# Differential scores in four row groups, operand transposes by single bank, a 96-row block in the query expansion

## The chip, the cores and the metric

The kernel runs on one core of a Trainium2 chip. The metric is the device time of one execution in microseconds (us). Engines are named as the profile has them: PE is TensorE, DVE is VectorE, ACT is ScalarE, POOL is GpSimd, SP is SyncE.

## What is computed

A hybrid encoder trunk of two layers works on two groups of 256 tokens of 1024 channels that share all parameters. Each layer projects the normed input into columns for four token mixers "a" to "d" and their gates, runs the mixers, merges them by sigmoid gates, projects, and ends in a gated MLP. The change touches the differential mixer "a", the operands of "c" and "d", and the query expansion of "c":

```python
def diff_mixer(cols, ang, lq1, lk1, lq2, lk2, subln, lam_init):
    q, k, v = jnp.split(cols, [A_QK_COLS, 2 * A_QK_COLS], axis=-1)
    q = apply_rope(q.reshape(b, s, A_HEADS, 2, A_D), ang) * (A_D ** -0.5)
    k = apply_rope(k.reshape(b, s, A_HEADS, 2, A_D), ang)
    ...
        sc = jnp.einsum('bqhcd,bkhcd->bhcqk', qb, k).astype(f32)
        p = jax.nn.softmax(sc, axis=-1)
        w = (p[:, :, 0] - lam * p[:, :, 1]).astype(v.dtype)
        return jnp.einsum('bhqk,bkhd->bqhd', w, v)
    o = rmsnorm(o, subln) * (1.0 - lam_init)
...
def mla_mixer(cols, ang, q_norm, kv_norm, w_uq, w_ukv):
    cq, ckv, k_rope = jnp.split(cols, [C_QLORA, C_QLORA + C_KVLORA], axis=-1)
    q = (rmsnorm(cq, q_norm) @ w_uq).reshape(b, s, C_HEADS, C_NOPE + C_ROPE)
```

There are four "a" heads with two score maps each, of width A_D = 32; C_QLORA is 192, that is 128 rows and 64.

## The kernel before

Every fp32 matmul is made of three fp32r matmuls on split operands: a value is written as a high part `h` and a low part `l`, and a product is hh + hl + lh (`mm3`, L297 to L299). The weights come in 264 pieces: an SP queue loads `raw`, ACT rounds it to `wh` (L289), and DVE and POOL share the rest `wl` (L292, L293). 512 tokens, both groups, lie in the free dimension.

The work is a list of units, one for a column of weights, in the order b, a, d, c of the mixers and then the gates; a unit's matmuls take a PSUM bank (`psum`), and an evacuation follows a unit later. Side generators run a step at a time between units. `pair_gen(mix, b, j)` handles one pair of heads of one group: scores, softmax, transposes of the probabilities (`pt`, L808) and their evacuation (`ptr`, L814), then the product with the values (`po`, L862). `cd_gen` makes the operands of "c" and "d" from token-major columns by transposing them on TensorE (L558). The program order of all this is then rearranged by a scheduler, so which instruction stands before which on an engine is seen only in the order of the built kernel.

PSUM has 8 banks of 512 columns: `pm` has four, for all main products (`psak`, `psva`, `psvd`, `pg`, `tr`, `cq`); `psx` two, for scores (`sc`); `pst` one, for `pt`; `pso` one, for `po`. A bank's next use waits until its last reader is done.

- *Mixer "a".* `a_evac` takes a finished product of 128 rows (four maps of 32), rotates it (`rc`, `rsh`, POOL has a part), splits it into `h` and `l`, and then stacks, for each of the four maps, three 32-row slices into one 96-row operand (`aq0p`, ...): h, h, l for queries against h, l, h for keys, so that one matmul of 96 rows gives all three terms. Of the 12 slice copies of an operand, four go to ACT (`APACK`, L604) and eight to DVE (L606). The scores of a head's two maps are 2 matmuls each (L738), and the two heads of a pair follow at different steps.
- *Mixers "b" and "d"* use `scores_rows` (L755 to L766): two heads lie in rows 0 to 63 and 64 to 127, and their 12 matmuls alternate between the two row groups (L765). "b" adds a bias on DVE right from the score bank (`sb`, L776).
- *The query expansion* `cq_pe` (L635 to L637) multiplies per 128 tokens a 128-row block and a 64-row block (`c0`, `c1`) of 384 columns.
- POOL also makes row tables for "d" (`rt`, from L474 on), at the time of the "b" pairs.

Of the kernel before, what the change touches and what calls it, by code (L numbers as in the profile page):

```python
# [30 lines left out]
APACK = (0, 3, 6, 9)  # L31
# [171 lines left out]
def trunk_kernel(ctx: ExitStack, tc: tile.TileContext, xt, wflat, gains, lams, rpb, consts, yt):  # L203
# [232 lines left out]
    def build_layer(l):  # L436
# [85 lines left out]
        def cd_gen():  # L522
# [30 lines left out]
            for i in range(0, 6, 2):  # L553
                pss = []
                for nm, src, a, m, g in jobs[i:i + 2]:
                    ps = psum("tr")
                    for t in range(4):
                        PE.transpose(out=ps[:m, t * 128:t * 128 + 128], in_=att[src][t][:, a:a + m], identity=ident)  # L558
                    pss.append(ps)
                yield  # L560
                for ps, (nm, src, a, m, g) in zip(pss, jobs[i:i + 2]):
                    h, lo = t2(nm + "h", F32R), t2(nm + "l", F32R)
                    if g is None:
                        split(ps[:m], h[:m], lo[:m])
                    else:
                        gc = gcol(l, g, 0, m)
                        S.activation(out=h[:m], in_=ps[:m], func=AF.Copy, scale=gc)
                        V.scalar_tensor_tensor(out=lo[:m], in0=ps[:m], scalar=gc, in1=f(h[:m]), op0=ALU.mult,
                                               op1=ALU.subtract)
                    att[nm] = (h, lo)  # L570
                yield
# [16 lines left out]
        def a_evac(nm):  # L588
            def evac():
                ps = D.pop(nm)  # L590
                c, sh = t2("rc"), t2("rsh")
                V.tensor_tensor(out=c, in0=ps, in1=st["cosr"], op=ALU.mult)
                V.stream_shuffle(out=sh, in_=ps, mask=SWAP)
                G.tensor_tensor(out=sh, in0=sh, in1=st["sinr"], op=ALU.mult)
                V.tensor_tensor(out=c, in0=c, in1=sh, op=ALU.add)
                h, lo = t2(nm + "h", F32R), t2(nm + "l", F32R)
                split(c, h, lo)
                parts = (h, h, lo) if nm[1] == "q" else (h, lo, h)
                for m in range(4):
                    pk = t2(f"{nm}p{m}", F32R)  # L600
                    r = slice(32 * m, 32 * m + 32)
                    for i, src in enumerate(parts):
                        if (3 * m + i) % 12 in APACK:
                            S.activation(out=pk[32 * i:32 * i + 32], in_=f(src[r]), func=AF.Copy)  # L604
                        else:
                            V.tensor_copy(out=pk[32 * i:32 * i + 32], in_=f(src[r]))  # L606
                    att[nm, m] = pk
# [19 lines left out]
        def cq_pe(wh, wl):  # L627
            w = [a[:, :768].rearrange("p (k c) -> p k c", k=2) for a in (wh, wl)]
            att["cqr"] = []
            for t in range(4):  # L630
                ps = psum("cq")
                o = ps[:, :384]
                for k, m in ((0, 128), (1, 64)):
# [87 lines left out]
        def heads(mix, j):  # L721
            if mix == "a":
                return [[((f"aq{j}", 2 * e + c), (f"ak{j}", 2 * e + c), 0, 96) for c in range(2)] for e in range(2)]
# [8 lines left out]
        def scores(maps, b):  # L732
            out = []
            for qn, kn, p0, n in maps:
                ps = psum("sc", psx)
                if isinstance(qn, tuple):
                    for qt in range(2):
                        PE.matmul(ps[:, qt * 256:qt * 256 + 256],  # L738
                                  lhsT=att[qn][0:96, b * 256 + qt * 128:b * 256 + qt * 128 + 128],
                                  rhs=att[kn][0:96, b * 256:b * 256 + 256], start=True, stop=True)  # L740
                    out.append(ps)
                    continue
# [12 lines left out]
        def scores_rows(maps, b):  # L755
            pss = [psum("sc", psx) for _ in maps]
# [75 lines left out]
        def pair_gen(mix, b, j):  # L832
            hs = heads(mix, j)
            rows = mix in "bd"
            if rows:
                s0, s1 = ([ps] for ps in scores_rows([hs[0][0], hs[1][0]], b))
# [456 lines left out]
```

## Time and profile before

| | |
|---|---|
| time, median of 3 runs | 1647.43 us (1647.31 to 1648.04) |
| the profiled execution, its own time | 1647.62 us |
| span of its trace | 1645.8 us |
| mean granted clock of TensorE | 0.989 |
| busy: PE / DVE / POOL / ACT | 1615.6 / 1003.9 / 663.1 / 634.9 us |

The span is the time from the first to the last instruction in the trace. A matmul's busy time includes its way through the array, so the matmuls of a full pipe overlap in the listing, and the distance of two starts says how long one occupies the engine. A granted clock of 1.00 is the 2.4 GHz level, 0.50 the 1.2 GHz level. A figure in brackets behind an instruction is the idle time of its engine just before it, and what ended it.

### The profile page before, as it was taken

What the parts mean: (1) busy time and instruction counts of PE and PEld (TensorE: products, weight loads), DVE (VectorE), ACT (ScalarE), POOL (GpSimd) and SP (SyncE); (2) the same over time, 40 slices, a digit from 0 to 9 for tenths busy, and PEclk for the clock granted to TensorE, in tenths of its full rate; (3) what the DMA queues carried; (4) which work ended last, traced back from release to release, by engine and by line L of the source; (5) the groups of instructions that cost most, each with busy time, mean ns of one, the idle gap of its engine ahead of it and who ended that gap; (6) DMA issues with size and microseconds to landing.
All of it is one profiled execution on the core that took longest, in us unless ns stands there. A gap on an engine that the chain in (4) does not pass through costs nothing.

```text
span 1645.8 us, 21201 instructions
## 1 busy us (share of the span) xinstructions
PE 1615.6 (98%) x8035; PEld 1343.8 (82%) x8035; DVE 1003.9 (61%) x1668; ACT 634.9 (39%) x1115; POOL 663.1 (40%) x449
## 2 busy tenths in 40 slices
PE   8989999999999999999998999999999999999997
PEld 6889877878888888888886987888788888888886
DVE  7787585655776666633358675756468666656113
ACT  4555553342323333322234554544333333333321
POOL 4352223444634444444444312234465344444342
PEclk9999999999999999999998999999999999999999
DMA  6222122222323322323331121322222233232331
GB/s 218 84 68 82 55 96 80 80 78 70 107 90 103 98 95 91 98 93 106 101 109 67 55 94 57 108 84 80 77 72 98 90 103 103 90 98 88 106 95 63
DMA packets 50534, 149.24 MB, mean 91 GB/s; under 512 B 13184, under 2 KB 16128, under 8 KB 50432
## 3 DMA queue, kind: packets, MB, share of 16 engines
q1 hardware_dynamic: 49344, 146.84, 27.4%
q8 instruction: 63, 1.03, 0.3%
q10 hardware_dynamic: 1088, 1.05, 0.2%
q14 instruction: 39, 0.32, 0.1%
HBM read 145.77 MB, written 2.10 MB: 90 GB/s over the span
## 4 chain that ended last, share of the span: by engine, by line
PE 93%; DVE 3%; issue 2%; ACT 1%; POOL 0%; DMA 0%; SPq 0%; POOLq 0%; ACTq 0%; DVEq 0%
PE pf L298 10%; PE pf L299 10%; PE pf L297 10%; PE pg L297 7%; PE pg L298 7%; PE pg L299 7%; PE pfo L297 5%; PE pfo L298 5%; PE pfo L299 5%; PE pb L299 2%; PE pwo L299 2%; PE pb L298 2%; PE pwo L298 2%; PE pb L297 2%; PE pwo L297 2%
## 5 line engine op out<-in xcount | busy, mean ns | idle before, releaser
L293 POOL TENSOR_TENSOR wl<-raw,wh 128x512 fp32r<-128x512 f32 (+4 forms) x264 | 449.9, 1705 | 561.7 <-ACT wh L289 439.9
L289 ACT ACTIVATE wh<-raw 128x1024 fp32r<-128x1024 f32 (+5 forms) x264 | 281.7, 1068 | 436.4 <-PE pfo L298 132.3
L292 DVE TENSOR_TENSOR wl<-raw,wh 128x512 fp32r<-128x512 f32 (+4 forms) x262 | 254.1, 970 | 213.6 <-ACT wh L289 203.6
L297 PE MATMUL pf<-xh,wh 128*128 128x512 f32 x704 | 274.3, 390 | 0.0
L299 PE MATMUL pf<-xh,wl 128*128 128x512 f32 x704 | 273.9, 389 | 0.0
L298 PE MATMUL pf<-xl,wh 128*128 128x512 f32 x704 | 273.9, 389 | 0.0
L297 PE MATMUL pg<-xh,wh 128*128 128x512 f32 x512 | 202.2, 395 | 0.1
L298 PE MATMUL pg<-xl,wh 128*128 128x512 f32 x512 | 199.8, 390 | 0.0
L299 PE MATMUL pg<-xh,wl 128*128 128x512 f32 x512 | 199.5, 390 | 0.0
L297 PEld LDWEIGHTS pf<-xh,wh 128*128 128x128 f32 x704 | 132.2, 188 | 27.5
L298 PEld LDWEIGHTS pf<-xl,wh 128*128 128x128 f32 x704 | 132.2, 188 | 27.4
L299 PEld LDWEIGHTS pf<-xh,wl 128*128 128x128 f32 x704 | 132.2, 188 | 27.2
L297 PE MATMUL pfo<-ah,wh 128*128 128x512 f32 (+1 forms) x374 | 141.1, 377 | 0.0
L298 PE MATMUL pfo<-al,wh 128*128 128x512 f32 (+1 forms) x374 | 140.8, 376 | 0.0
L299 PE MATMUL pfo<-ah,wl 128*128 128x512 f32 (+1 forms) x374 | 140.8, 376 | 0.0
L931 POOL TENSOR_TENSOR mg<-mg,gz 128x512 f32<-128x512 f32 x48 | 64.5, 1347 | 165.4 <-DVE gz L930 165.4
L303 POOL TENSOR_TENSOR al<-fc,ah 128x512 fp32r<-128x512 f32 x44 | 57.8, 1314 | 178.9 <-ACT ah L302 178.9
L297 PEld LDWEIGHTS pg<-xh,wh 128*128 128x128 f32 x512 | 96.2, 188 | 21.1 <-issue 0.9
L299 PEld LDWEIGHTS pg<-xh,wl 128*128 128x128 f32 x512 | 96.1, 188 | 20.5
L298 PEld LDWEIGHTS pg<-xl,wh 128*128 128x128 f32 x512 | 96.3, 188 | 18.3
L952 ACT ACTIVATE gz<-gz 128x512 f32<-128x512 f32 x64 | 40.4, 631 | 127.3 <-DVE gz L951 127.2
L788 ACT ACTIVATE pr<-sc,mx 128x256 f32<-128x256 f32 x128 | 59.1, 471 | 78.6 <-DVE mx L783 78.6
(390 smaller groups left out, 2917.5 us busy)
## 6 DMA issues: line engine op xcount, KB each, us to landing
raw<-in_w_dram SPq DMA_DIRECT2D x158, 512.0 KB, 3.3
raw<-in_w_dram SPq DMA_DIRECT2D x58, 640.0 KB, 3.8
raw<-in_w_dram SPq DMA_DIRECT2D x32, 448.0 KB, 3.3
raw<-in_w_dram SPq DMA_DIRECT2D x4, 576.0 KB, 3.4
bias<-in_rpb_dram SPq DMA_DIRECT2D x32, 64.0 KB, 3.5
xall<-in_xt_dram SPq DMA_DIRECT2D x3, 512.0 KB, 7.1
raw<-in_w_dram SPq DMA_DIRECT2D x4, 256.0 KB, 4.5
out_dram<-y SPq DMA_DIRECT2D x4, 256.0 KB, 2.5
```

The source lines that it names most:

```text
L289: S.activation(out=wh[:, a:b], in_=raw[:, a:b], func=AF.Copy)
L292: V.tensor_tensor(out=wl[:, a:c], in0=raw[:, a:c], in1=f(wh[:, a:c]), op=ALU.subtract)
L293: G.tensor_tensor(out=wl[:, c:b], in0=raw[:, c:b], in1=f(wh[:, c:b]), op=ALU.subtract)
L297: PE.matmul(ps, lhsT=wh, rhs=xh, start=first, stop=False)
L298: PE.matmul(ps, lhsT=wh, rhs=xl, start=False, stop=False)
L299: PE.matmul(ps, lhsT=wl, rhs=xh, start=False, stop=last)
L303: (eng or V).tensor_tensor(out=l, in0=v, in1=f(h), op=ALU.subtract)
L788: S.activation(out=p[:, qt * 256:qt * 256 + 256], in_=src[c][:, qt * 256:qt * 256 + 256], func=AF.Exp, scale=sc, bias=mx[:, i:i + 1], accu ...
L931: G.tensor_tensor(out=m, in0=m, in1=z, op=ALU.add)
L952: S.activation(out=z, in_=z, func=AF.Tanh, scale=0.5)
```

## The change

`a_evac` stops at the split `h` and `l`; the stacked operands and their copies are gone. The scores of an "a" pair go through `scores_rows`: four maps, each in its own 32 rows, take 24 matmuls (3 terms, 2 query tiles, 4 maps) in one go. The banks of maps 0 and 1 come from `psx`, those of maps 2 and 3 from `pm`. `cd_gen` transposes and splits its six operands one at a time, each in a step of its own, instead of two at a time. The second block of `cq_pe` has 96 rows; the added rows meet weights that are zero. The functions touched stand in a diff of the source:

```diff
--- before.py
+++ after.py
@@ -28,7 +28,6 @@
 RPB_W = 128
 ORD = 'badc'
 GSEQ = [(i, d) for i in ('abcd'.index(m) for m in ORD) for d in range(ND)]
-APACK = (0, 3, 6, 9)
 NWARM = 9
 BLAG = 5
 GX = [(25, 29), (31, 32)]
@@ -550,24 +549,20 @@
                 yield
             jobs = (("dk", "dr", 288, 128, None), ("dq0", "dr", 32, 128, None), ("dq1", "dr", 160, 128, None),
                     ("c2", "cf", 0, 128, G_CKV), ("c0", "cf", 128, 128, G_CQ), ("c1", "cf", 256, 96, G_CQ + 1))
-            for i in range(0, 6, 2):
-                pss = []
-                for nm, src, a, m, g in jobs[i:i + 2]:
-                    ps = psum("tr")
-                    for t in range(4):
-                        PE.transpose(out=ps[:m, t * 128:t * 128 + 128], in_=att[src][t][:, a:a + m], identity=ident)
-                    pss.append(ps)
+            for nm, src, a, m, g in jobs:
+                ps = psum("tr")
+                for t in range(4):
+                    PE.transpose(out=ps[:m, t * 128:t * 128 + 128], in_=att[src][t][:, a:a + m], identity=ident)
                 yield
-                for ps, (nm, src, a, m, g) in zip(pss, jobs[i:i + 2]):
-                    h, lo = t2(nm + "h", F32R), t2(nm + "l", F32R)
-                    if g is None:
-                        split(ps[:m], h[:m], lo[:m])
-                    else:
-                        gc = gcol(l, g, 0, m)
-                        S.activation(out=h[:m], in_=ps[:m], func=AF.Copy, scale=gc)
-                        V.scalar_tensor_tensor(out=lo[:m], in0=ps[:m], scalar=gc, in1=f(h[:m]), op0=ALU.mult,
-                                               op1=ALU.subtract)
-                    att[nm] = (h, lo)
+                h, lo = t2(nm + "h", F32R), t2(nm + "l", F32R)
+                if g is None:
+                    split(ps[:m], h[:m], lo[:m])
+                else:
+                    gc = gcol(l, g, 0, m)
+                    S.activation(out=h[:m], in_=ps[:m], func=AF.Copy, scale=gc)
+                    V.scalar_tensor_tensor(out=lo[:m], in0=ps[:m], scalar=gc, in1=f(h[:m]), op0=ALU.mult,
+                                           op1=ALU.subtract)
+                att[nm] = (h, lo)
                 yield
 
         def swap_h():
@@ -595,16 +590,7 @@
                 V.tensor_tensor(out=c, in0=c, in1=sh, op=ALU.add)
                 h, lo = t2(nm + "h", F32R), t2(nm + "l", F32R)
                 split(c, h, lo)
-                parts = (h, h, lo) if nm[1] == "q" else (h, lo, h)
-                for m in range(4):
-                    pk = t2(f"{nm}p{m}", F32R)
-                    r = slice(32 * m, 32 * m + 32)
-                    for i, src in enumerate(parts):
-                        if (3 * m + i) % 12 in APACK:
-                            S.activation(out=pk[32 * i:32 * i + 32], in_=f(src[r]), func=AF.Copy)
-                        else:
-                            V.tensor_copy(out=pk[32 * i:32 * i + 32], in_=f(src[r]))
-                    att[nm, m] = pk
+                att[nm] = (h, lo)
             return evac
 
         def b_evac(nm):
@@ -630,7 +616,7 @@
             for t in range(4):
                 ps = psum("cq")
                 o = ps[:, :384]
-                for k, m in ((0, 128), (1, 64)):
+                for k, m in ((0, 128), (1, 96)):
                     h, lo = (a[:m, t * 128:t * 128 + 128] for a in att[f"c{k}"])
                     PE.matmul(o, lhsT=h, rhs=w[0][:m, k], start=(k == 0), stop=False)
                     PE.matmul(o, lhsT=h, rhs=w[1][:m, k], start=False, stop=False)
@@ -720,7 +706,7 @@
 
         def heads(mix, j):
             if mix == "a":
-                return [[((f"aq{j}", 2 * e + c), (f"ak{j}", 2 * e + c), 0, 96) for c in range(2)] for e in range(2)]
+                return [[(f"aq{j}", f"ak{j}", 32 * (2 * e + c), 32) for c in range(2)] for e in range(2)]
             if mix == "b":
                 return [[(f"bq{j}", f"bk{j}", 64 * e, 64)] for e in range(2)]
             if mix == "c":
@@ -733,13 +719,6 @@
             out = []
             for qn, kn, p0, n in maps:
                 ps = psum("sc", psx)
-                if isinstance(qn, tuple):
-                    for qt in range(2):
-                        PE.matmul(ps[:, qt * 256:qt * 256 + 256],
-                                  lhsT=att[qn][0:96, b * 256 + qt * 128:b * 256 + qt * 128 + 128],
-                                  rhs=att[kn][0:96, b * 256:b * 256 + 256], start=True, stop=True)
-                    out.append(ps)
-                    continue
                 (qh, ql), (kh, kl) = att[qn], att[kn]
                 ks = slice(b * 256, b * 256 + 256)
                 p = slice(p0, p0 + n)
@@ -753,7 +732,7 @@
             return out
 
         def scores_rows(maps, b):
-            pss = [psum("sc", psx) for _ in maps]
+            pss = [psum("sc", psx if i < 2 else pm) for i in range(len(maps))]
             ks = slice(b * 256, b * 256 + 256)
             for qt in range(2):
                 qs = slice(b * 256 + qt * 128, b * 256 + qt * 128 + 128)
@@ -831,9 +810,10 @@
 
         def pair_gen(mix, b, j):
             hs = heads(mix, j)
-            rows = mix in "bd"
+            rows = mix in "abd"
             if rows:
-                s0, s1 = ([ps] for ps in scores_rows([hs[0][0], hs[1][0]], b))
+                ss = scores_rows(hs[0] + hs[1], b)
+                s0, s1 = ss[:len(ss) // 2], ss[len(ss) // 2:]
             else:
                 s0 = scores(hs[0], b)
             yield
```

The order of the built kernels shows three places. On VectorE, in the stage of the second "b" head of layer 1, before (`aq1h` and `aq1l` are the split query operand, `sb` the bias addition that frees a score bank, `ob0l` an output's low part):

```order
L303 TENSOR_TENSOR aq1l_848<-rc_841,aq1h_847 128x512
L606 CAST aq1p0_851<-aq1h_847 32x512
L606 CAST aq1p0_851<-aq1l_848 32x512
L606 CAST aq1p1_855<-aq1h_847 32x512
L606 CAST aq1p1_855<-aq1l_848 32x512
L606 CAST aq1p2_859<-aq1h_847 32x512
L606 CAST aq1p2_859<-aq1l_848 32x512
L606 CAST aq1p3_863<-aq1h_847 32x512
L606 CAST aq1p3_863<-aq1l_848 32x512
L303 TENSOR_TENSOR ob0l_875<-po_819,ob0h_874 128x256
L776 SCALAR_TENSOR_TENSOR sb_909<-sc_781,bias3_242 128x512
L592 TENSOR_TENSOR rc_918<-psak1_794,cosr_373 128x512
```

And after, from the line ahead of `aq1l` on:

```order
L777 TENSOR_SCALAR sb_800<-sb_800,ri_799 128x256 x2
L302 TENSOR_TENSOR aq1l_816<-rc_809,aq1h_815 128x512
L291 TENSOR_TENSOR wl12_881<-raw12_683,wh12_880 128x576
L302 TENSOR_TENSOR ob0l_827<-po_787,ob0h_826 128x256
L755 SCALAR_TENSOR_TENSOR sb_861<-sc_749,bias3_242 128x512
L587 TENSOR_TENSOR rc_870<-psak1_762,cosr_373 128x512
```

The eight casts between the query's low part and `sb` are gone; the weight residue `wl12`, which stood ahead of the reciprocal before, now stands there with `ob0l`.

On TensorE, in the gate stage of layer 1 (`pg` a gate column, `tr` a transposed operand in a main bank, `dr` the token-major columns), before:

```order
L298 MATMUL pg_1704<-xl7_169,wh18_1510 128x512
L299 MATMUL pg_1704<-xh7_168,wl18_1511 128x512
L558 MATMUL tr_1754<-cst_82,dr0_896 128x128
L558 MATMUL tr_1754<-cst_82,dr1_897 128x128
L558 MATMUL tr_1754<-cst_82,dr2_898 128x128
L558 MATMUL tr_1754<-cst_82,dr3_899 128x128
L558 MATMUL tr_1759<-cst_82,dr0_896 128x128
L558 MATMUL tr_1759<-cst_82,dr1_897 128x128
L558 MATMUL tr_1759<-cst_82,dr2_898 128x128
L558 MATMUL tr_1759<-cst_82,dr3_899 128x128
L297 MATMUL pg_1764<-xh0_122,wh19_1689 128x512
L298 MATMUL pg_1764<-xl0_123,wh19_1689 128x512
```

And after:

```order
L297 MATMUL pg_1672<-xl7_169,wh18_1462 128x512
L298 MATMUL pg_1672<-xh7_168,wl18_1463 128x512
L555 MATMUL tr_1722<-cst_82,dr0_848 128x128
L555 MATMUL tr_1722<-cst_82,dr1_849 128x128
L555 MATMUL tr_1722<-cst_82,dr2_850 128x128
L555 MATMUL tr_1722<-cst_82,dr3_851 128x128
L296 MATMUL pg_1727<-xh0_122,wh19_1663 128x512
L297 MATMUL pg_1727<-xl0_123,wh19_1663 128x512
L298 MATMUL pg_1727<-xh0_122,wl19_1664 128x512
```

One transposed operand stands between two gate columns instead of two; `pg_1727` takes the main bank that the first "a" pair's last map (`sc_1473`) had.

On TensorE, later in the gate stage of layer 1, around the start of the fourth "a" pair's scores, before (`po` is the product with the values, in two row groups and two key tiles):

```order
L299 MATMUL pg_1982<-xh7_168,wl22_1897 128x512
L862 MATMUL po_2010<-ptr_1819,vA_88 64x256
L862 MATMUL po_2010<-ptr_1903,vA_88 64x256
L862 MATMUL po_2010<-ptr_1819,vA_88 64x256
L862 MATMUL po_2010<-ptr_1903,vA_88 64x256
L808 MATMUL pt_2015<-cst_82,pr_1884 128x128 x4
L738 MATMUL sc_2030<-ak1p0_928,aq1p0_851 128x256 x2
L738 MATMUL sc_2033<-ak1p1_932,aq1p1_855 128x256 x2
L297 MATMUL pg_2036<-xh0_122,wh23_1975 128x512
```

And after:

```order
L787 MATMUL pt_1841<-cst_82,pr_1703 128x128 x4
L555 MATMUL tr_1877<-cst_82,dr0_848 128x128
L555 MATMUL tr_1877<-cst_82,dr1_849 128x128
L555 MATMUL tr_1877<-cst_82,dr2_850 128x128
L555 MATMUL tr_1877<-cst_82,dr3_851 128x128
L842 MATMUL po_1972<-ptr_1778,vA_88 64x256
L744 MATMUL sc_2001<-ak1h_876,aq1h_815 128x256
L744 MATMUL sc_2002<-ak1h_876,aq1h_815 128x256
L842 MATMUL po_1972<-ptr_1875,vA_88 64x256
L842 MATMUL po_1972<-ptr_1778,vA_88 64x256
L296 MATMUL pg_1882<-xh0_122,wh21_1769 128x512
```

Before, the four `po` matmuls stand together and four score matmuls follow; now three `po` matmuls stand around two score matmuls (of 24), the fourth `po` and the other 22 come behind the gate column.

## Rows read from the trace of the kernel before

**Rows 1.** Page, busy time of the engines and their instructions.

```profile
PE 1615.6 (98%) x8035; PEld 1343.8 (82%) x8035; DVE 1003.9 (61%) x1668; ACT 634.9 (39%) x1115; POOL 663.1 (40%) x449
```

**Rows 2.** TensorE's waits: line, releaser, us in total, times, longest.

```profile
PE sc L765 <- DVE sb L776: 9.3, 4, 3.1
PE pt L808 <- ACT ptr L814: 4.4, 2, 2.2
```

**Rows 3.** Timeline, TensorE, layer 1: start, us, instruction, count, idle before and releaser.

```profile
73.14 1.56 PE L862 MATMUL po<-ptr,vB 128*64 128x256 f32 x8
...
74.63 0.66 PE L808 MATMUL pt<-cst,sb 128*128 128x128 f32 x4
...
86.39 0.66 PE L808 MATMUL pt<-cst,sb 128*128 128x128 f32 x4 [2.19 <-ACT ptr L814]
...
90.81 0.58 PE L765 MATMUL sc<-bk1h,bq1h 64*128 64x256 f32 x1 [3.05 <-DVE sb L776]
...
92.98 0.41 PE L457 MATMUL psvd<-wh,xl 128*128 128x256 f32 x1
93.19 0.41 PE L455 MATMUL psvd<-wh,xh 128*128 128x256 f32 x1
...
99.95 1.08 PE L862 MATMUL po<-ptr,vB 128*64 128x256 f32 x8
```

**Rows 4.** Timeline, TensorE, layer 2, the same stretch.

```profile
884.45 0.66 PE L808 MATMUL pt<-cst,sb 128*128 128x128 f32 x4
...
910.88 1.08 PE L862 MATMUL po<-ptr,vB 128*64 128x256 f32 x8
```

**Rows 5.** Windows: busy us of each engine in 5 us, then TensorE's clock.

```profile
90.00:95.00 5.00, 4.19 (x18) 3.97 (x19) 3.50 (x9) 1.57 (x6) 1.28 (x1) 0.50 0.00 0
```

**Rows 6.** VectorE: one group of casts by line; then the timeline.

```profile
L606 DVE CAST aq1p<-aq1h 32x512 fp32r<-32x512 f32 x8 | 5.4, 671 | 0.1
...
90.08 0.68 DVE L776 SCALAR_TENSOR_TENSOR sb<-sc,bias 128x512 f32<-128x512 f32 x1
```

**Rows 7.** Timeline, TensorE, scores among value matmuls.

```profile
135.16 0.28 PE L455 MATMUL psva<-wh,xh 128*128 128x256 f32 x1
135.28 0.28 PE L456 MATMUL psva<-wl,xh 128*128 128x256 f32 x1
135.40 0.44 PE L738 MATMUL sc<-ak0p,aq0p 96*128 96x256 f32 x2
135.68 0.28 PE L457 MATMUL psva<-wh,xl 128*128 128x256 f32 x1
```

**Rows 8.** Chain of waits, TensorE: start, us, name, line, count.

```profile
146.35 0.44 PE pt L808 x4
...
152.74 0.87 PE tr L558 x8
...
161.56 0.48 PE sc L738 x4
...
205.23 0.91 PE sc L765 x12
```

**Rows 9.** Timeline, GpSimd, row tables.

```profile
81.32 0.68 POOL L474 COPY rt<-cst 128x32 f32<-128x32 f32 x1
...
87.84 1.58 POOL L477 TENSOR_TENSOR rt<-cst,lv 128x256 f32<-128x256 f32 x2
```

**Rows 10.** Timeline, TensorE, starts of two blocks of the query expansion.

```profile
206.06 0.44 PE L635 MATMUL cq<-wh,c0h 128*128 128x384 f32 x1
...
206.79 0.44 PE L635 MATMUL cq<-wh,c1h 64*128 64x384 f32 x1
```

**Rows 11.** Timeline, VectorE and ScalarE, softmax of the first "a" pair.

```profile
142.05 0.18 DVE L791 RECIPROCAL ri<-su 128x4 f32<-128x4 f32 x1 [2.48 <-ACT pr L788]
...
153.11 1.28 DVE L782 TENSOR_REDUCE mx<-sc 128x2 f32<-128x512 f32 x2
...
155.70 0.47 ACT L788 ACTIVATE pr<-sc,mx 128x256 f32<-128x256 f32 x1 [2.04 <-DVE mx L783]
```

## The prediction, made before the changed kernel was run

> **What bounds the kernel now.** I read the page first: TensorE is busy for 98% of the span, VectorE for 61% [rows 1]. With an engine that full, a change can only gain where TensorE idles, where it runs slowly, or where work is taken off it, and it can lose wherever a new wait is put ahead of it. So the second view is the table of TensorE's waits. Only two of them are more than a microsecond: score matmuls of the "b" mixer (L765) that wait for `sb` on VectorE, 9.3 us in four waits, and transposes of its probabilities (L808) that wait for `ptr` on ScalarE, 4.4 us in two [rows 2]. The third view, TensorE's timeline, shows where these lie: all in one stretch per layer, between the first "b" pair's transposes and the next `po` group, 74.63 to 99.95 us in layer 1 [rows 3] and 884.45 to 910.88 us in layer 2 [rows 4]. The reader is to see there two more things. The matmuls behind a stall are spaced 0.21 us apart instead of 0.12 us, and the windows give the slice from 90 to 95 us a granted clock of 0.50, which is the 1.2 GHz level [rows 3, 5]. So each stall is paid twice, once idle and once at half clock.
>
> Why does TensorE wait there? The second "b" head needs a score bank of PSUM, of which there are two, and a bank is free only when VectorE has added the bias into `sb`. VectorE does this for the third score bank at 90.08 us [rows 6], and TensorE starts 0.7 us later [rows 3]. Ahead of it in VectorE's queue stand the eight casts that build the stacked operands of `aq1`, those from `aq1h` 0.67 us each on average [rows 6]; the order shown above has the same eight rows between `aq1l` and `sb`.
>
> **The change part by part.**
>
> *The stall of the "b" stage.* The change takes 64 casts off VectorE and 32 copies off ScalarE, four operands of each layer. What TensorE has to do between the two points is 96 matmuls of 256 columns at 0.1195 us [rows 7], or 11.5 us, two groups of scores at 0.91 us and two of transposes at 0.44 us [rows 8], and 0.2 us of small change: 14.4 us. The stretch lasts 25.32 us in layer 1 and 26.43 us in layer 2 [rows 3, 4], so 51.75 − 28.8 = 22.9 us is lost there, 13.7 us of it idle [rows 2] and the other 9.2 us at half clock. If I replay VectorE's queue without the casts, from the same durations, `sb` of the second head is ready near 76.1 us where TensorE wants it near 77.3 us, a margin of 1.2 us. What is late next is GpSimd: its row tables run from 81.32 to 89.4 us [rows 9] and hold its part of the rotary product, so VectorE gets the rotated operand at about 85 us, and the bank of `psvd` comes free at about 88 us where TensorE wants it at 90.6 us. So I expect the whole 22.9 us: **−22.9**. With no wait the first `po` group, which now lasts 1.56 us in one place and 1.08 us in the other [rows 3], should be short in both layers: **−1.0**.
>
> *The query expansion.* In `cq` a block of three 384-column matmuls takes 0.73 us from start to start [rows 10], where at the steady rate it would be 3 × 1.5 × 0.1195 = 0.54 us. It alternates between 128 rows and 64 rows, so each change of form costs about 0.19 us. A 96-row pair in a stream of 128-row matmuls costs no such step: two of them start at 135.40 us and the stream goes on at 135.68 us, 0.28 us for two matmuls [rows 7]. With 96 rows some seven of eight changes go, in two layers: 14 × 0.2 = **−2.8**. The extra rows add no columns.
>
> *The scores.* Eight pairs (four per layer) were two groups of four stacked matmuls, 0.48 us each [rows 8], 0.96 us a pair. Now they are 24 matmuls of 32 rows. The trace has no 32-row groups; the nearest row is two groups of 64 rows, twelve matmuls in 0.91 us with the mode changes, which is six times 0.12 us and 0.2 us: the two groups run beside each other [rows 8]. If four groups run beside each other, 24 matmuls are again six steps, 0.91 us, and I take that: 8 × (0.91 − 0.96) = **−0.4**. The other ends are two at a time, 12 × 0.12 + 0.2 = 1.6 us, and one at a time, 24 × 0.12 + 0.2 = 3.1 us; these are rivals below.
>
> The Trainium skill, "TensorE: Matmul & The Clock Gate", Part 3 (Packing small matmuls), gives 3.07× for four row tiles of K=32, less than the four that I take from the 64-row pair. By it, as an estimate, a pair would be 24 × 0.12 / 3.07 + 0.2 = 1.14 us, and the sum 1.8 us higher; no row here shows four tiles.
>
> *Split groups.* In the new order the fourth "a" pair and the first "d" pair are cut: part of `po`, two or three score matmuls, more of `po`, a whole gate column, and only then the rest. A cut means four more changes of form, of 0.19 us or less, and part of a `po` group that does not overlap: about 0.65 us for each of two places in each layer, **+2.6** (from 0.8 us, if changes overlap, to 4).
>
> *A new wait for a main bank.* Maps 2 and 3 of a pair take their banks from the pool of the main products. In the gate stage `pg` must then have the bank that the first "a" pair's last map held, and that is freed by the exponentials on ScalarE. In before the reciprocal `ri` is at 142.05 us, the maxima `mx` at 153.11 us, and the exponential `pr` at 155.70 us [rows 11], behind VectorE's queue of scalings and weight residues. By the replay of the new order VectorE has both maxima about a microsecond sooner, the two exponentials end near 154.9 us, and TensorE, which has only four transposes there instead of eight (0.87 us for eight [rows 8]), comes at 152.7 us. The wait is then 2.2 us per layer, **+4.4**. It is nothing if VectorE's queue is 2 us shorter than replayed, and 4 us if ScalarE does weights first. What queues behind it on TensorE is everything, since it works in order. After the stalls of the "b" stage the half clock cost 9.2 us for six stalls [rows 2, 5], 1.5 us for one; whether a single stall among full columns brings it is not shown, so I take half of it for two layers, **+1.5** (0 to 3.1). Other small waits for the two main banks that are left (`psva`, `tr`, `pg` alternate on them, with margins of 0.6 to 0.9 us in the replay): **+0.5**.
>
> *The transposes one bank at a time.* They are the same 24 per layer, in six steps instead of three. They end before `cq` starts in either order, so I cost them at nothing; what hides the splitting of each is the gate column in between, 24 matmuls of 512 columns or 24 × 2 × 0.1195 = 5.7 us of TensorE work. Without that cover a transposition wait would be at most the 0.4 us of four transposes a step.
>
> **The sum.** −22.9 − 1.0 − 2.8 − 0.4 + 2.6 + 4.4 + 1.5 + 0.5 = −18.1 us. The profiled execution took 1647.6 us (its span is 1645.8 us), 0.2 us over the median of the runs shown: 1647.6 − 18.1 = **1629.5 us**. Its own range is 1623.5 us, with no wait for the main bank (−4.4 − 1.5), to 1634.7 us, with 4 us each and all of the half clock (+3.6 + 1.6).
>
> **The rivals.**
>
> *A, the main banks become the bound.* Two of four are held by scores through a softmax, and each of two further columns per layer waits some 2 us as well: 1629.5 + 2 × 2 × 1.8 = 1637 us (1634 to 1641). For it: the margins of 0.6 to 0.9 us above. Against it: a column is 5.7 us long, and a bank is wanted once in a column. The Trainium skill, "TensorEngine Tiling (Array Packing)", Gotcha 1 (PSUM Pressure), says that different row tiles write to different banks, so two banks could not do; no run here shows it yet. Chance 0.15.
>
> *B, row groups overlap only two at a time.* 1.6 us instead of 0.91 us in eight pairs: +5.5, 1635 us. The only overlap in the trace is of two [rows 8]. Chance 0.10.
>
> *C, the slower side: row groups run one after another, at the half clock.* Few rows at work could bring the 1.2 GHz level, as the stretch of the stalls has it [rows 5], and at its spacing of 0.21 us [rows 3] a pair would take 24 × 0.21 + 0.2 = 5.2 us: +4.3 × 8 = +34.6, about 1664 us. It decides from 3.2 us a pair (0.91 + 18.1 / 8), where the gain is gone. Against it: 64-row groups overlap [rows 8]. Chance 0.03.
>
> *D, the stall only moves.* GpSimd's row tables [rows 9] or a margin of 1.2 us lost leave one stall of 1.6 to 2 us with its half clock in each layer: +6 to 7, 1636 us. Chance 0.05.
>
> *E, the change doesn't do what it says*: `sb` is late for another reason (weight residues of VectorE), and the casts' time goes to those. About 1647 us. Chance 0.03.
>
> **How the numbers follow.** The forecast has the remaining 0.64. The range from 1622 to 1638 us holds nine tenths of it (0.58), half of A (0.08), B and D: 0.81. Differences within 0.2%, 3.3 us, are about what a measurement of this kernel can tell from none. Faster by more are the forecast, A, B and D, 0.94; the same is E, 0.03; slower is C, 0.03.
>
> **What would show it.** The waits L765 on `sb` and L808 on `ptr` should be gone from the table of waits, and the windows from 75 to 95 us should have clock 1.00; if a wait of over a microsecond stands there, the replay was wrong. In `cq` the blocks should start 0.54 us apart. The 24 score matmuls of an "a" pair should take 0.9 to 1.1 us; 1.6 us is B. A new row `pg <- ACT pr` should stand among the waits, some 2 us long, twice; several of them are A, and none at all would put the time near 1623.5 us.

## The result, and the profile after

The changed kernel takes **1635.91 us** (median of 4 runs, 1633.07 to 1636.70), beside 1647.67 us for the kernel before: a ratio of 0.9925, with a 95% interval from 0.9908 to 0.9943. Measured again in a later group of runs it took 1634.30 us (1632.39 to 1635.81, 5 runs) beside 1647.38 us, 0.9921 (0.9909 to 0.9934). The time is lower by 12 to 13 us, where 18.1 us were forecast; it lies inside the range from 1622 to 1638 us, near its upper end. The forecast's own range, up to 1634.7 us, holds the second of these times and not the first.

The page of the changed kernel, line 1 of busy time (engine, us, share, instructions), answers to [rows 1]. VectorE lost 64 instructions and 36 us; TensorE has more matmuls, and is busy for 99%:

```profile
PE 1612.5 (99%) x8163; PEld 1338.6 (82%) x8163; DVE 968.2 (59%) x1604; ACT 614.2 (38%) x1083; POOL 661.8 (41%) x449
```

TensorE's waits after, the longest sums first (releaser, us in total, times, longest), answer to [rows 2]. Both waits of the "b" stage are gone; on top stands a wait that the kernel before does not have, a gate column for ScalarE's `pr`; the second is the first weights' at the start of the program:

```profile
PE pg L296 <- ACT pr L767: 4.5, 2, 2.3
PE psbk L296 <- ACT wh L288: 2.7, 1, 2.7
```

The windows after over the stretch where the stall was (busy us of each engine, then TensorE's clock) answer to [rows 5]. TensorE is busy throughout, at clock 1.00:

```profile
75.00:80.00 5.00, 5.00 (x38) 4.04 (x35) 4.64 (x10) 1.91 (x4) 3.77 (x6) 1.00 0.15 21
80.00:85.00 5.00, 5.00 (x44) 5.00 (x43) 0.77 (x2) 1.46 (x5) 4.56 (x9) 1.00 0.27 112
...
90.00:95.00 5.00, 5.00 (x41) 4.34 (x40) 4.74 (x10) 3.92 (x10) 3.88 (x3) 1.00 0.32 102
```

Where the time went is read from the starts of five pieces of work on TensorE's timeline: the "b" pair's `po` ahead of the stall, the first `psve`, the first `psva`, the first `cq`, and the gate column behind the query expansion. Layer 1 before (the first and the fourth also stand in [rows 3, 10]):

```profile
101.38 0.38 PE L455 MATMUL psve<-wh,xh 128*128 128x288 f32 x1
...
134.01 0.36 PE L455 MATMUL psva<-wh,xh 128*128 128x256 f32 x1
...
212.17 0.48 PE L297 MATMUL pg<-xh,wh 128*128 128x512 f32 x1
```

And the same pieces of layer 1 after:

```profile
74.47 1.08 PE L842 MATMUL po<-ptr,vB 128*64 128x256 f32 x8
...
91.64 0.38 PE L454 MATMUL psve<-wh,xh 128*128 128x288 f32 x1
...
125.00 0.39 PE L454 MATMUL psva<-wh,xh 128*128 128x256 f32 x1
...
203.24 0.44 PE L621 MATMUL cq<-wh,c0h 128*128 128x384 f32 x1
...
208.22 0.47 PE L296 MATMUL pg<-xh,wh 128*128 128x512 f32 x1
```

The differences of these starts, and of the same ones in layer 2, give the length of each stretch in us:

| stretch | layer 1 before | after | layer 2 before | after |
|---|---|---|---|---|
| `po` to `psve` (the stall) | 28.24 | 17.17 | 29.33 | 17.17 |
| `psve` to `psva` | 32.63 | 33.36 | 32.63 | 33.36 |
| `psva` to `cq` (gate stage) | 72.05 | 78.24 | 72.04 | 76.59 |
| `cq` to the gate column | 6.11 | 4.98 | 6.10 | 4.99 |

So the stall gives 23.2 us and the query expansion 2.2 us, as forecast to within a microsecond; but `psve` to `cq` takes 6.9 us more in layer 1 and 5.3 us more in layer 2, 12.2 us, which is half of the gain. The second and the third row are to be taken together: of the four "a" pairs of a layer the second one's scores, about 1 us, stand behind the first `psva` before and ahead of it after. Everything behind (the rest of the gates, the output, the MLP) is the same to 0.2 us. The first `po` of the profiled execution comes 1.3 us later than before; in the profiles of other kernels here it comes from 72.9 to 74.7 us, in a second profile of the changed kernel at 73.2 us, so this is scatter of the start and no part of the change. Of the 1.3 us some 0.9 us are longer waits for the first weights (2.7 and 0.7 us instead of 1.9 and 0.5 us).

### The profile page after: what moved, and what is told of

The parts are those of the page before. It is cut to its first block, busy times and chain, and to the rows that moved or that the text cites. A ratio compares the mean times of both kernels' runs of the same rounds, so it can differ in the third digit from the quotient of the medians.

```text
span 1633.6 us, 21325 instructions
## 1 busy us (share of the span) xinstructions
PE 1612.5 (99%) x8163; PEld 1338.6 (82%) x8163; DVE 968.2 (59%) x1604; ACT 614.2 (38%) x1083; POOL 661.8 (41%) x449
## 4 chain that ended last, share of the span: by engine, by line
PE 95%; DVE 3%; ACT 1%; issue 1%; DMA 0%; POOL 0%; SPq 0%; POOLq 0%; ACTq 0%; DVEq 0%
PE pf L297 10%; PE pf L296 10%; PE pf L298 10%; PE pg L296 7%; PE pg L297 7%; PE pg L298 7%; PE pfo L296 5%; PE pfo L297 5%; PE pfo L298 5%; PE po L842 2%; PE pt L787 2%; PE pb L298 2%; PE pwo L298 2%; PE pb L296 2%; PE pb L297 2%; PE pwo L297 2%
## 5 line engine op out<-in xcount | busy, mean ns | idle before, releaser
L296 PEld LDWEIGHTS pg<-xh,wh 128*128 128x128 f32 x512 | 96.5, 188 | 28.2 <-ACT pr L767 5.0
```

The lines of the kernel that those rows point to most:

```text
L296: PE.matmul(ps, lhsT=wh, rhs=xh, start=first, stop=False)
```

## The experiments

In the order of the questions: was it the casts, where does the gate stage lose, and what are the other two parts worth. Lengths of stretches are taken from the profiles as in the table above.

**The casts alone put back.** The changed kernel, with the copies of the operands made again (their results are not read):

```diff
                 att[nm] = (h, lo)
+                parts = (h, h, lo) if nm[1] == "q" else (h, lo, h)
+                for m in range(4):
+                    pk = t2(f"{nm}p{m}", F32R)
...
+                            S.activation(out=pk[32 * i:32 * i + 32], in_=f(src[r]), func=AF.Copy)
...
+                            V.tensor_copy(out=pk[32 * i:32 * i + 32], in_=f(src[r]))
             return evac
```

> The changed kernel with the 8 VectorE casts and 4 ScalarE copies of each "a" operand put back in their old place; what they write is not read, the scores stay in four row groups. If the casts in VectorE's queue were what held the second "b" head (my theory), the waits of the "b" scores on sb and of the transposes on ptr come back, 6.8 us of idle time per layer, with the half clock behind them, and the time is 1636 + 23 = 1659 us (1654 to 1662). If the stall went because the scores have another form or place, the casts cost next to nothing and the time stays at 1633 to 1638 us.

Measured: 1655.56 us (1654.93 to 1655.81, 4 runs), 1.0049 (1.0034 to 1.0065) of the kernel before. Its waits:

```profile
PE sc L754 <- DVE sb L765: 9.3, 4, 3.1
PE pg L297 <- ACT pr L777: 4.5, 2, 2.3
PE pt L797 <- ACT ptr L803: 4.4, 2, 2.2
```

The first and the third are those of [rows 2] to the tenth, and the stretch from `po` to `psve` is back at 28.2 and 28.0 us. The stall hangs on these copies and on nothing else of the change; VectorE's casts and ScalarE's copies were put back together, so what each of them does is not parted. What is left over, 8 us above the kernel before, is in the main the 12.1 us that `psve` to `cq` takes more, less 2.2 us of the query expansion and 1.4 us by which the two stalls together are shorter.

**The banks of the two heads exchanged.** In the changed kernel maps 0 and 1 take the main banks, maps 2 and 3 the score banks:

```diff
-            pss = [psum("sc", psx if i < 2 else pm) for i in range(len(maps))]
+            pss = [psum("sc", pm if len(maps) == 4 and i < 2 else psx) for i in range(len(maps))]
```

> The changed kernel with the score banks of an "a" pair swapped: maps 0 and 1, whose softmax comes first, take the main banks, and maps 2 and 3 the score banks. If the wait of pg on pr and the cut po groups both come from main banks that are held through the second softmax (my theory), the wait of 2 x 2.25 us goes or falls under 2 x 0.5 us, its half clock goes too, po stands whole again, and the time is 1636 - 4 - 2 - 3 = 1627 us (1625 to 1630). If the extra time of the gate stage is the price of the row groups themselves (changes of form) or of the transposes in six steps, only the wait goes: 1630 to 1632 us. If any two main banks held are as bad as the others, 1634 to 1637 us.

Measured: 1627.19 us (1626.07 to 1627.71, 4 runs), 0.9878 (0.9864 to 0.9891). The wait of `pg` on `pr` is gone, every `po` group stands whole, and the gate stage is down to 71.4 us in layer 1 and 72.9 us in layer 2, where the half clock came (told at the end). But the stretch ahead of it grew from 33.4 to 35.1 us. TensorE's timeline shows why: the second pair's score matmuls came out two at a time and then one at a time (x2 and x1, starts 0.12 us apart), and take 2.9 us from the first to the next `psva`:

```profile
122.23 0.38 PE L744 MATMUL sc<-ak0h,aq0h 32*128 32x256 f32 x2
...
123.91 0.27 PE L744 MATMUL sc<-ak0l,aq0h 32*128 32x256 f32 x1
...
125.14 0.39 PE L454 MATMUL psva<-wh,xh 128*128 128x256 f32 x1
```

I took it that its score banks are still held by the first pair's second softmax, which the next kernel bears out: there the pieces are whole.

**The same, with the first pair as in the change.**

```diff
-        def scores_rows(maps, b):
-            pss = [psum("sc", psx if i < 2 else pm) for i in range(len(maps))]
+        def scores_rows(maps, b, swap=False):
+            pss = [psum("sc", pm if len(maps) == 4 and (i < 2) == swap else psx) for i in range(len(maps))]
...
-                ss = scores_rows(hs[0] + hs[1], b)
+                ss = scores_rows(hs[0] + hs[1], b, b + j > 0)
```

> The changed kernel with the banks swapped (maps 0 and 1 in main banks) for the last three "a" pairs of a layer, and as in the change for the first. In the run with all four swapped, the second pair's 24 score matmuls came out in pieces, 2.9 us instead of 1.0 us, because its score banks were still held by the first pair's second softmax; here they stand whole in the order, as does every po group. If the loss of the gate stage is all from held banks (my theory), the stage is back at the length it had before the change, and the time is 1635 - 2 x 5.25 - 1.6 = 1623 us (1622 to 1625). If a part is the row groups' own or that of the transposes in six steps, 1626 to 1628 us.

Measured: **1624.74 us** (1624.28 to 1625.63, 4 runs), 0.9861 (0.9847 to 0.9874): 23 us faster than before, and the fastest kernel here. The gate stage takes 72.65 and 72.61 us where it took 72.05 and 72.04 us before, and `psve` to `cq` 106.0 us in both layers against 104.7 us. One wait of 1.1 us per layer is left, for the gate product that frees the same bank on VectorE:

```profile
PE pg L296 <- DVE gz L931: 2.3, 2, 1.1
```

Of the 12.2 us that `psve` to `cq` took more, 2.6 us are left, and 2.2 us of them are this wait. So nearly all of the loss came from which banks the maps hold, and when; a price of the row groups themselves, which was the other reading, would have stayed.

**The two costs apart.** In the kernel just shown the condition for the exchange is narrowed, first to the second pair, then to the third and fourth:

```diff
-                ss = scores_rows(hs[0] + hs[1], b, b + j > 0)
+                ss = scores_rows(hs[0] + hs[1], b, (j, b) == (0, 1))
```

> The changed kernel with the banks swapped for the second "a" pair alone, the one whose last map holds the main bank that a gate column waits for. In the order the po groups and the scores behind them stay cut in the same two places of each layer. If the wait and the cuts are two separate costs (my theory), the wait of 2 x 2.25 us becomes one of VectorE's gate product of 2 x 1.1 us, the half clock behind it goes mostly, and the cuts stay: 1635 - 2.2 - 1.6 = 1631 us (1630 to 1632.5). If the cuts cost nothing of their own and their time is that of the wait, 1625 us as with three pairs swapped.

Measured: 1630.62 us (1629.74 to 1631.64, 4 runs), 0.9899 (0.9885 to 0.9914). The wait is one of 1.1 us per layer for `gz`, as in the kernel with three pairs exchanged; the cuts are there. The gate stage takes 75.29 and 75.26 us, 2.65 us per layer more than without cuts.

```diff
-                ss = scores_rows(hs[0] + hs[1], b, b + j > 0)
+                ss = scores_rows(hs[0] + hs[1], b, j == 1)
```

> The changed kernel with the banks swapped for the third and the fourth "a" pair of a layer alone. In the order every po group and every pair's 24 score matmuls stand whole, and the second pair's last map still holds the main bank for the gate column. If the wait and the cuts are two separate costs (my theory), the wait of 4.5 us in two places stays, with its half clock in one layer, and the cuts' 2.9 us per layer go: 1635 - 5.7 = 1629.5 us (1628 to 1631). If the cuts cost only the 1.3 us per layer of the prediction, 1632 to 1633 us.

Measured: 1630.11 us (1628.78 to 1630.64, 4 runs), 0.9897 (0.9881 to 0.9914). No cuts, and the wait of `pg` on `pr` in full, 4.5 us in two places. The gate stage takes 74.01 us in one layer and 75.60 us in the other; the difference is the half clock behind the wait, told below. In the layer without it the cuts make 76.59 − 74.01 = 2.58 us. The two costs are separate and add up.

**The changed kernel again.**

> The changed kernel once more, unchanged, beside the others. Its runs so far lie from 1633.1 to 1636.7 us with mean clocks from 0.997 down to 0.993. If the half clock behind the wait of pg on pr (seen in layer 1 of the profiled run, not in layer 2) comes in neither, one or both layers, each is worth 1.7 us, and times and clocks fall into such steps: about 1633, 1635 and 1636.5 us. If the scatter is that of the first weight transfers, the clock doesn't go with the time.

Measured: 1634.30 us (1632.39 to 1635.81, 5 runs). The time goes with the clock over all nine runs of this kernel: those with a mean clock of 0.997 or 0.998 took 1632.4 to 1633.2 us, those with 0.995 took 1634.3 to 1635.8 us, and those with 0.993 took 1636.5 and 1636.7 us. That fits the half clock in neither, one or both layers, but does not show it: the mean clock also holds the start and the end of the program, and the kernel with the first pair as in the change has 0.995 in its profile without any half clock in the gate stages. In the profile of this run the gate stage takes 78.23 and 76.60 us, so again one layer has it.

**The query expansion alone undone.**

```diff
-                for k, m in ((0, 128), (1, 96)):
+                for k, m in ((0, 128), (1, 64)):
```

> The changed kernel with the second block of the query expansion at 64 rows again. By the traces (a block's start to the next 0.73 us against 0.53 us, 8 blocks in a layer) it costs 2 x 1.1 to 2 x 1.5 us: 1638 to 1639 us, and the blocks start 0.71 to 0.73 us apart. If the rows of a block set its time, nothing is lost or some is won: 1634 to 1636 us.

Measured: 1636.90 us (1636.31 to 1639.41, 4 runs), under the 1638 to 1639 us expected, since the changed kernel beside it took 1634.30 us and not 1636; the difference of 2.6 us is as expected, though the scatter of both leaves it uncertain by more than a microsecond. The stretch is sharper: 6.11 and 6.12 us, against 4.98 and 4.99 us. Two starts of blocks in the timeline, 0.72 us apart, with 0.73 us in [rows 10]:

```profile
200.22 0.44 PE L621 MATMUL cq<-wh,c0h 128*128 128x384 f32 x1
...
200.94 0.44 PE L621 MATMUL cq<-wh,c1h 64*128 64x384 f32 x1
```

With 96 rows the first two blocks of the changed kernel start 0.63 us apart (203.24 and 203.87 us), the next ones 0.54 and 0.52 us.

**The scores left stacked**, that is the kernel before with only the transposes one at a time and the 96 rows (the edits are those of the change).

> The kernel before with the other two parts of the change alone: the transposes one at a time and the second block of the query expansion at 96 rows; the scores stay stacked and the casts stay. By the traces of the changed kernel the query expansion gives 1.1 us in each layer and the transposes nothing: 1647.5 - 2.2 = 1645 us (1644 to 1646). If the transposes in six steps cost something of their own (a step more for each bank, behind a gate column), 1646 to 1649 us; if they take a share in the gain, under 1644 us.

Measured: 1645.05 us (1643.57 to 1645.95, 11 runs), 0.9982 (0.9974 to 0.9991), 2.6 us under the kernel before. The query expansion has 4.98 us in both layers, the gate stage 72.12 and 72.11 us, as before: with stacked scores the six steps cost nothing.

**The transposes in pairs again**, the rest as changed (the edit is the change's second hunk, reversed).

> The changed kernel with the transposes two at a time as before. If main banks are what is short while a pair's scores hold two of four (my theory), two transposed operands at once leave none for the next gate column, TensorE waits more than the 4.5 us of the changed kernel, and the time is 1638 to 1642 us: the six steps are then there to pay for the banks. If the transposes don't matter to the banks, 1633 to 1636 us.

Measured: 1638.85 us (1638.42 to 1639.54, 4 runs), 0.9946 (0.9933 to 0.9960). The gate stage takes 80.00 and 79.75 us, and a second pair of waits has come, now before the transposes, since they take the banks:

```profile
PE tr L557 <- ACT pr L771: 4.5, 2, 2.3
...
PE tr L557 <- DVE gz L935: 2.1, 2, 1.1
```

So with row groups the six steps are worth 3 to 4.5 us, by which of the two times of the changed kernel is taken: they keep one main bank free where the scores hold two. Part of it is the half clock, 1.6 us a time, which came in both layers here (clock 0.66 from 145 to 150 us and from 950 to 955 us).

**Two row groups at a time.** The changed kernel, with the two heads of a pair scored at different steps again, from the score banks alone:

```diff
-            rows = mix in "abd"
+            rows = mix in "bd"
...
+            elif mix == "a":
+                s0 = scores_rows(hs[0], b)
...
-                s1 = scores(hs[1], b)
+                s1 = scores_rows(hs[1], b) if mix == "a" else scores(hs[1], b)
```

> The changed kernel with the two heads of an "a" pair at different steps, as before: two row groups of 32 rows at a time, 12 matmuls, banks from the score pool alone. No main bank is held, so the wait of pg on pr and the cut groups should be gone (-4.5 - 1.6 - 6 us), and each pair costs 2 x 0.92 us instead of 0.97 us (+7 us): 1630 us (1628 to 1632). If two groups at a time bring the half clock or new waits for the two score banks, over 1635 us.

Measured: 1640.05 us (1638.27 to 1642.96, 4 runs), 0.9956 (0.9941 to 0.9971): 10 us over the main expectation; it was the other branch, with new waits for the score banks, that came. Twelve matmuls with two groups do take 0.90 us (106.17 to 107.07 us), as reckoned. But in two heads of each layer the two score banks were not free together, so the maps ran one after the other, with a wait for the first:

```profile
111.02 0.38 PE L744 MATMUL sc<-ak0h,aq0h 32*128 32x256 f32 x1 [1.10 <-ACT pr L767]
...
112.28 0.38 PE L744 MATMUL sc<-ak0h,aq0h 32*128 32x256 f32 x1
```

The forecast had counted the matmuls and not the banks: with two banks and two maps a head the softmax is on the path. The stretch from `psve` to `cq` is 7.8 and 6.3 us longer than in the 1624.7 us kernel, 14.1 us together. The second half of eight pairs, at 0.9 us, makes 7.2 us of it, four heads in pieces some 0.9 us more each, 3.6 us, the two waits 2.2 us, and the half clock behind the wait of layer 1 (0.80 from 110 to 115 us and 0.86 from 115 to 120 us) 1.5 us, the difference of the two layers. These make 14.5 us, 0.4 us more than was measured.

## Why the prediction was right, and where it was off, point by point

| term | forecast, us | measured, us | from |
|---|---|---|---|
| stall of the "b" stage, with its `po` | −23.9 | −23.2 | `po` to `psve`, both layers |
| query expansion | −2.8 | −2.2 | `cq` to the gate column |
| scores | −0.4 | about 0 | whole pairs 0.91, 1.10 and 0.92 us, where 0.96 us stood before |
| cut groups | +2.6 | +5.2 to 5.3 | 2.58 and 2.65 us per layer, in the two runs that part the costs |
| wait for the main bank | +4.4 | +4.5 | the wait of `pg` on `pr` |
| its half clock | +1.5 | +1.6 | one of two layers of the profiled run |
| small waits and the rest of the stage | +0.5 | +0.8 | what is left of 12.2 us |
| start of the program | 0 | +1.3 | scatter of the profiled run |

The measured terms make −12.0 us, and the spans of the two profiles differ by 12.2 us. The forecast was 18.1 us. That the first measurement, 1635.91 us, still lies in the range is owed to the width that rivals A, B and D gave it, and none of the three came.

**The stall** went as the replay said: no wait stands between `po` and `psve`, and the two layers, 1.1 us apart before, take the same 17.17 us. The third `sb`, at 90.08 us before [rows 6], is at 77.19 us, done at 77.87 us, and TensorE takes the bank at 78.56 us; the replay had it ready at 76.1 us and wanted at 77.3 us, which with the later start of 1.3 us is 77.4 and 78.6 us. The margin is so 0.7 us and not 1.2 us, and it was enough. Rivals D and E fell with this. One reading in the prediction was too short: three more waits of TensorE are over a microsecond before, 1.4 and 1.9 us at the start of the program and 2.5 us at its end (`rb` for `ny`); the change has no part in them.

**The scores.** Four row groups do run beside each other. TensorE's timeline of the third pair, after, with four matmuls in each line:

```profile
154.73 0.39 PE L744 MATMUL sc<-ak1h,aq1h 32*128 32x256 f32 x4
154.96 0.29 PE L744 MATMUL sc<-ak1l,aq1h 32*128 32x256 f32 x4
155.07 0.29 PE L744 MATMUL sc<-ak1h,aq1l 32*128 32x256 f32 x4
155.19 0.29 PE L744 MATMUL sc<-ak1h,aq1h 32*128 32x256 f32 x4
155.31 0.29 PE L744 MATMUL sc<-ak1l,aq1h 32*128 32x256 f32 x4
155.43 0.29 PE L744 MATMUL sc<-ak1h,aq1l 32*128 32x256 f32 x4
...
155.65 0.50 PE L296 MATMUL pg<-xh,wh 128*128 128x512 f32 x1
```

Six steps of 0.12 us and a change of form, 0.92 us from the first to the gate column. That is the extrapolation from two groups [rows 8]; rivals B and C fall. The first pair takes 0.91 us (106.65 to 107.56 us); the second takes 1.10 us (123.90 us to `psva` at 125.00 us), and why it does is not known. By the Trainium skill's 3.07× for four row tiles ("TensorE: Matmul & The Clock Gate", Part 3, Packing small matmuls) it would have been, as an estimate, 1.14 us; here the rows decide, and those of the first and the third pair show the full four.

**The new wait** was foreseen in its place and size. TensorE's timeline after, in layers 1 and 2:

```profile
145.39 0.50 PE L296 MATMUL pg<-xh,wh 128*128 128x512 f32 x1 [2.27 <-ACT pr L767]
...
949.94 0.50 PE L296 MATMUL pg<-xh,wh 128*128 128x512 f32 x1 [2.27 <-ACT pr L767]
```

The bank is one of the second "a" pair; the part ahead of the prediction, the prediction and [rows 11] call this pair the first. The first pair's last exponential starts at 125.27 us, and with the second pair's banks alone exchanged this wait went. ScalarE begins the exponentials that free the bank here:

```profile
144.32 0.47 ACT L767 ACTIVATE pr<-sc,mx 128x256 f32<-128x256 f32 x1 [5.60 <-DVE mx L762]
```

The half clock behind it was taken at half of two layers for want of a row, so that it came in one of two is luck: 0.66 in layer 1, 1.00 in layer 2, after the same wait. Windows after:

```profile
145.00:150.00 5.00, 4.61 (x13) 3.65 (x14) 3.71 (x8) 3.21 (x9) 1.29 (x1) 0.66 0.59 214
...
949.00:954.00 5.00, 4.06 (x18) 3.37 (x19) 3.17 (x8) 3.76 (x11) 1.31 (x1) 1.00 0.60 222
```

**The step that failed is the cut groups**, the term of the sum that was mis-sized most: 1.3 us per layer forecast, 2.6 us measured. I priced a cut as mode changes and part of a `po`. The rows of the first cut, after, show more:

```profile
162.21 0.65 PE L842 MATMUL po<-ptr,vA 128*64 128x256 f32 x2
162.79 0.38 PE L744 MATMUL sc<-ak1h,aq1h 32*128 32x256 f32 x2
163.10 0.65 PE L842 MATMUL po<-ptr,vA 128*64 128x256 f32 x4
163.68 0.50 PE L296 MATMUL pg<-xh,wh 128*128 128x512 f32 x1
...
175.28 0.65 PE L842 MATMUL po<-ptr,vA 128*64 128x256 f32 x2
175.86 0.66 PE L787 MATMUL pt<-cst,pr 128*128 128x128 f32 x4
176.35 0.60 PE L555 MATMUL tr<-cst,cf 128*128 128x128 f32 x4
176.88 0.38 PE L744 MATMUL sc<-ak1h,aq1h 32*128 32x256 f32 x2
...
177.99 0.50 PE L296 MATMUL pg<-xh,wh 128*128 128x512 f32 x1
```

A piece of two or four `po` matmuls takes 0.58 us by itself, where a whole group of eight takes 1.01 us: three pieces make 1.74 us. Two lone scores take 0.31 us and the rest of the pair 1.11 us instead of 0.92 us. Together the cut place takes 1.47 + 2.71 = 4.18 us, and the same work whole takes 2.95 us in the kernel with the first pair as in the change:

```profile
170.31 1.08 PE L842 MATMUL po<-ptr,vA 128*64 128x256 f32 x8
171.32 0.66 PE L787 MATMUL pt<-cst,pr 128*128 128x128 f32 x4
171.82 0.60 PE L555 MATMUL tr<-cst,cf 128*128 128x128 f32 x4
172.35 0.39 PE L744 MATMUL sc<-ak1h,aq1h 32*128 32x256 f32 x4
...
173.26 0.50 PE L296 MATMUL pg<-xh,wh 128*128 128x512 f32 x1
```

1.2 us for this place, 1.0 us for the other (185.51 to 187.10 and 201.29 to 203.24 us, 3.54 us, against 2.50 us whole before), and the remaining 0.4 us per layer is not assigned. The cut itself was seen in the order before the run; its cause was not: exchanging the banks of the last two pairs makes it go, which suggests that the scheduler cuts where a bank is not yet free by its own reckoning; that reckoning itself is not shown.

**The transposes** were costed at nothing, with the gate columns as cover. With stacked scores that holds; beside row groups they are needed, and what they need is a free bank and not time to hide in. The prediction had the banks as rival A, "the main banks become the bound"; that came out as one wait per layer and not three.

**The query expansion** gave 1.1 us per layer instead of 1.4 us, because not seven but about six changes' worth of 0.19 us went: the blocks that follow other matmuls, the first and the fifth, still take 0.63 and 0.60 us.

## What to carry to other kernels

When work is taken off an engine that holds back a full TensorE, look up which wait comes next in PSUM: banks borrowed from another pool are free again only when their last reader is through, so give the borrowed ones to the maps that are read first. Four row groups of 32 are worth it here if all four can start together, which needs four free banks at once. Where the order cuts a group of concurrent matmuls, each piece costs more than its share: two or four of eight `po` matmuls took 0.58 us, the eight together 1.01 us. So price a cut by its pieces, not by its changes of form.

## What the runs showed of the hardware that was not expected

*GpSimd was slower beside VectorE's casts.* The last row table of layer 1 took 0.79 us for each of its products before [rows 9]; the same products after, with no casts beside them, take 0.59 us:

```profile
82.12 1.18 POOL L476 TENSOR_TENSOR rt<-cst,lv 128x256 f32<-128x256 f32 x2
```

With the casts put back the 1.58 us for two are there again:

```profile
88.65 1.58 POOL L477 TENSOR_TENSOR rt<-cst,lv 128x256 f32<-128x256 f32 x2
```

All the row tables together take 5.1 us (78.17 to 83.30 us) instead of 8.1 us, where rival D had them at their old length; whether the stall would have moved on to them at that length was not tried. The casts were slowed as well: before, five of them from 73.94 us on, with GpSimd idle, took 0.42 us each, and the eight from 84.49 us on, beside the row tables, took 0.42 to 0.85 us. Why the two engines hinder each other is not shown.

*The half clock comes without a wait, too.* In the kernel with all four pairs' banks exchanged TensorE waited nowhere in the "a" stage, yet behind the 2.9 us of matmuls with one or two row groups at work the clock fell in layer 2 (the window below, 0.74), and not in layer 1 behind the same work:

```profile
926.00:931.00 5.00, 5.00 (x33) 5.00 (x33) 1.11 (x4) 2.16 (x8) 0.00 (x0) 0.74 0.21 81
```

In five profiles with the wait of 2.27 us before a gate column it was followed by the half clock in exactly one of the two layers, in two of them in layer 1; in the profile with that wait before the transposes, in both layers. Behind the waits of 1.1 us before a gate column, in two profiles, it did not come; in the kernel with two row groups at a time it came in layer 1 behind a wait of 1.10 us and scores of one row group at a time, and not in layer 2 behind the same. It is worth 1.5 to 1.6 us a time.
